# Down's first eight left factors in four rooms, and up's first two pairs in turn over T2 and T1

## The chip, the cores and the metric

The kernel runs on one core of one Trainium2 chip. The metric is device time of one execution in microseconds (us), from the first to the last instruction with what the runtime puts around it. Five engines work side by side, each through its own row of instructions in a fixed order: TensorE (PE in the profile; its weight loads are PEld), VectorE (DVE), ScalarE (ACT), GpSimd (POOL) and SyncE (SP, which only issues transfers here). They wait for each other by semaphores.

## What is computed

Two layers over 1024 positions of width 1024, all in float32. Each layer has a mixer (a recurrent one in layer 0, attention in layer 1) and then a feed-forward part with a causal convolution of three taps. The change touches only the second:

```python
def conv_ffn(x, w_up, conv_w, conv_b, w_down):
    hid = causal_dwconv(x @ w_up, conv_w, conv_b)      # 1024 -> 2 x 2816
    gate, val = jnp.split(hid, 2, axis=-1)
    return (jax.nn.gelu(gate) * val) @ w_down          # 2816 -> 1024
...
    x = x + rms_norm(mix, g[1])
    h = rms_norm(x, g[2])
    x = x + rms_norm(conv_ffn(h, ffn_w_up[l], ...), g[3])
```

## The kernel before

**A float32 product in three.** Each float32 number is split into a high part (a cast on ScalarE) and a low part (the number less the high part, on DVE or POOL). `mm3` then makes a product of three matmuls of 128x512: high by high (L187), high by the low part of the moving side (L188), low part of the weights by high (L189). So the high parts are wanted first, the low parts one and two matmuls later. The split stands at several lines: L395 and L396 in `combined` for factors of the weights of up, L436 and L437 in `split_k` for the operands T, L481 and L482 for the products made ahead, L183 and L184 in `split` for the factors of down.

**Seven products for eight.** Both matrix products of the feed-forward part are taken as 2 by 2 blocks with seven products in place of eight. The price is sums and differences of blocks: the operands T1 to T4 of the normalized input, the factors s1 = a21 + a22, s2 = s1 - a11, a11 - a21 and a12 - s2 of the weights (`mixed`, L401, s1 and a11 - a21 on POOL, the others on DVE), and in down differences of blocks of w_down (L659) and of the hidden part (L540 to L543 in `sums`).

**up** works through 22 blocks n of 128 gate or value channels, a gate and its value in turn. For the first six (`AHEAD`), two of the seven products need only the first half of the input. They are made ahead, while the norm of the second half is still under way ("the products made ahead", L476 to L496), for three pairs of blocks one after another: four weight tiles of a pair are cast on ScalarE, their low parts are made on DVE, and the results are parked in DRAM. After that a block n < 6 has five products: y by T2, a copy of y to u2 (ScalarE, L579), z by T1, a copy q, y by T3, `second()` (a sum of y and q on DVE, L568), z by b22, `third()` (L572), y by T4. Then follow the convolution (L461 on ScalarE, two taps on DVE at L463), gelu on ScalarE (L615), the product of gate and value (L621) and `sums`. T2 and T1 are made before the first block, T3, b22 and T4 from inside it (`rest`, L526). A block n from 6 on has seven products. Its factors are asked for one block ahead (`factors(n + 1)`, `ahead()`).

**down** is 6 x 11 and then some more steps of 12 matmuls. A step has a left factor, 128x512 of the hidden part, read back from DRAM (`fetch`, tiles ar) and split, and a right factor from w_down (tiles hl). `make` prepares steps in order, three ahead of the step that runs, and starts with the loads (SP), then the difference of w_down (L659), then the split of the left and of the right factor. The left factors of the first four steps have rooms of their own in a large tile called ring, from the pool of large tiles (four of them, `hpool`); it is taken before the last blocks of up. From step 4 on the left factor goes to one of four rooms called al, which are taken when down opens its rooms (`open_rows`), after the last sums of up.

Besides the loops, the tile scheduler fixes each engine's order when the program is built, so that an instruction of another line can come to stand ahead of or behind the one written first. What stands in the rows around the change is shown below.

Of the kernel before, what the change touches and what calls it, by code (L numbers as in the profile page):

```python
# [26 lines left out]
FT = DFF // P  # L27
# [13 lines left out]
def hybrid_kernel(  # L41
# [56 lines left out]
    def bank(name):  # L98
        return psp.tile([P, HT], F32, tag="b4", name=name, bufs=4)

    def pj():
        return psp.tile([P, HT], F32, tag="pj", name="pj")
# [285 lines left out]

    def combined(raws, begun):

# [12 lines left out]

        s1 = mixed(pool, a21, a22, ALU.add)
        if begun:
            s2 = mixed(dve, s1, a11, ALU.subtract)
            yield split_of(s2, dve)
            yield split_of(s1, dve)
            yield split_of(mixed(pool, a11, a21, ALU.subtract), dve)
            yield split_of(mixed(dve, a12, s2, ALU.subtract), dve)  # L410
            yield split_of(a22, dve)
            return
# [9 lines left out]
    def up(l, hb, load_first, begin_down):  # L422
# [15 lines left out]

        def raw(f, s, i):
            own = s == 0 and "uraw" in pools  # L440
            name = "uraw" if own else "raw"
            t = (pools["uraw"] if own else rawp).tile([P, 4, P], F32, tag=name, name=name)
            nc.sync.dma_start(out=t, in_=w_up[l, s * FT + f, i].rearrange("p (k c) -> p k c", k=4))
            return t
# [30 lines left out]
        for n in range(0, AHEAD, 2):  # L475
            ws = [[], []]  # L476
            for i in range(2):
                for e, f in enumerate(order[n : n + 2]):
                    a = raw(f, 0, i)
                    w = wp.tile([P, 2, 4, P], F32R, tag="hl", name="hl")  # L480
                    act.copy(w[:, 0], a)  # L481
                    dve.tensor_tensor(out=w[:, 1], in0=a, in1=w[:, 0].bitcast(F32), op=ALU.subtract)  # L482
                    ws[e].append(w)
# [16 lines left out]
        def factors(n):  # L500
            f = order[n]
            return combined([raw(f, s, i) for s in range(2) for i in range(2)], n < AHEAD)

        ws = factors(0)
        early = [next(ws) for _ in range(2)]
        t2, t1, b22 = (operand(True) for _ in range(3))
# [20 lines left out]
        others = rest()  # L527
        next(others)

# [16 lines left out]
        def begin(n):  # L546
# [4 lines left out]
            return p1, c1  # L551

        g0 = None
        for n, f in enumerate(order):
            if n == FT - 4:
                load_first()
            more = factors(n + 1) if n + 1 < FT else begin_down()
            take, nxt = iter(early), []

            def ahead():  # L560
                nxt.append(next(more))

            y, z = pj(), bank("z")
            u2, q, c2 = tap("u2"), tap("q"), room("c")

            def second():

                dve.tensor_tensor(out=c2[:, first[1]], in0=y, in1=q, op=ALU.add)  # L568

# [4 lines left out]
            if n < AHEAD:  # L574
                p1, c1 = begin(n)
                act.copy(y, p1)
                w = next(ws)
                product(y, next(take), t2, False)
                act.copy(u2, y)  # L579
                w2 = next(ws)  # L580
                product(z, next(take), t1, True)
                act.copy(q, z)
                w3 = next(ws)
                next(others, None)
                product(y, w, t3, False)
                second()
                ahead()
                next(others, None)
                product(z, w2, b22, False)
                third()  # L590
                ahead()
                next(others, None)
            else:
# [23 lines left out]
            act.copy(c2[:, first[0]], y)  # L617
            if n + 1 >= AHEAD:
                ahead()
# [6 lines left out]
    def down(l, xsrc, dst, tail, primed):  # L626
# [76 lines left out]
        def make():  # L703
# [19 lines left out]
            r = raws.pop(i)  # L723
            a = st["ring"][:, i] if i < 4 else st["al"][i % 4]
            w_ = r.shape[-1]
# [1006 lines left out]
```

## Time and profile before

| | |
|---|---|
| median of 3 runs | 2436.53 us (2436.25 to 2438.01) |
| the profiled execution | 2437.43 us |
| its span, first to last instruction | 2435.7 us (1.73 around it) |
| granted TensorE clock, mean | 0.986 |
| busy: PE, PEld | 2328.8 us (96%), 1905.0 us (78%) |
| busy: DVE, ACT, POOL | 1917.9 us (79%), 1320.2 us (54%), 390.3 us (16%) |
| instructions | 32154 |
| moved by DMA | 279.08 MB, mean 115 GB/s |

Some places on the profile's clock, counted from the span's start: in layer 0 the products made ahead begin at 439.6, T2's first difference on DVE at 470.4, down with its first matmuls before 899.3; in layer 1 the same are at 1759.3, 1786.0 and before 2214.3.

A row of a timeline has the start, the duration, engine, line and operation, then the tile written, the tiles read (buffer numbers left out), their shape, and the count of instructions that the row takes together. In square brackets stands the idle time before it and what ended it. The granted clock (PEclk) is 1.00 where TensorE ran at full pace. A matmul's duration is longer than its distance to the next one, since matmuls overlap in the pipeline.

### The profile page before, as it was taken

To read this page: it belongs to the slowest core of one execution; us is meant where nothing else is said; L and a number is where in the kernel's file an instruction comes from. 1 tells how busy PE (TensorE), PEld (TensorE's weight loads), DVE (VectorE), ACT (ScalarE), POOL (GpSimd) and SP (SyncE) were. 2 spreads that over 40 slices of the span, in tenths; PEclk is the share of its full clock that TensorE was granted. 3 is DMA by queue.
4 is the path that set the end of the run, shared out by engine and by line. 5 is a ranking of instruction groups with operands and counts; after the bars stand their busy time and mean duration, and the time that the engine had idled before them with its cause. 6 is when DMAs were issued, how large, how long until landed. Compare 5 with 4: busy or idle time off the path is not lost.

```text
span 2435.7 us, 32154 instructions
## 1 busy us (share of the span) xinstructions
PE 2328.8 (96%) x10998; PEld 1905.0 (78%) x10998; DVE 1917.9 (79%) x3376; ACT 1320.2 (54%) x2440; POOL 390.3 (16%) x275
## 2 busy tenths in 40 slices
PE   8999999989999999998989999989989999999997
PEld 6888777767888878887778888877767788887886
DVE  6576776898888889586788888886988888887776
ACT  5343674655555545564556565565665555554453
POOL 2000000122333310000111111132031333330000
PEclk9999999999999999999999999999999999999999
DMA  4111125753233265433221121134665232237342
GB/s 140 35 33 38 40 80 169 242 171 119 92 120 113 91 206 172 129 124 120 64 54 45 50 53 52 52 90 126 229 200 180 98 119 104 91 122 262 113 152 94
DMA packets 145220, 279.08 MB, mean 115 GB/s; under 512 B 17600, under 2 KB 30048, under 8 KB 145056
## 3 DMA queue, kind: packets, MB, share of 16 engines
q1 hardware_dynamic: 143472, 272.66, 34.9%
q0 software_dynamic: 1440, 4.38, 0.6%
q8 instruction: 86, 1.41, 0.3%
q14 instruction: 78, 0.64, 0.1%
q10 hardware_dynamic: 144, 0.00, 0.0%
HBM read 200.36 MB, written 68.22 MB: 110 GB/s over the span
## 4 chain that ended last, share of the span: by engine, by line
PE 51%; DVE 15%; ACT 4%; issue 4%; DMA 2%; POOL 1%; SPq 0%; ACTq 0%; DVEq 0%; POOLq 0%
PE pj L187 8%; PE pj L189 8%; PE pj L188 8%; PE z L187 4%; PE z L189 4%; PE z L188 4%; PE x L189 2%; PE x L187 2%; DVE nm L1443 2%; PE x L188 2%; ACT pl L1453 2%; DVE pt L184 2%; PE tr L189 1%; PE tr L187 1%; PE tr L188 1%
## 5 line engine op out<-in xcount | busy, mean ns | idle before, releaser
L187 PE MATMUL pj<-op,hl 128*128 128x512 f32 x704 | 280.0, 398 | 18.8 <-ACT u L579 9.9
L188 PE MATMUL pj<-op,hl 128*128 128x512 f32 x704 | 278.2, 395 | 6.6 <-DVE op L437 6.4
L189 PE MATMUL pj<-op,hl 128*128 128x512 f32 x704 | 277.2, 394 | 3.4 <-DVE hl L482 3.4
L463 DVE SCALAR_TENSOR_TENSOR y<-c,cw,y 128x1023 f32<-128x1023 f32 (+1 forms) x176 | 230.6, 1311 | 6.4 <-ACT y L461 4.8
L187 PE MATMUL pj<-hh,hl 128*128 128x512 f32 x544 | 228.4, 420 | 0.3 <-DVE offs L1290 0.3
L189 PE MATMUL pj<-hh,hl 128*128 128x512 f32 x544 | 213.7, 393 | 0.0
L188 PE MATMUL pj<-hl,hl 128*128 128x512 f32 x544 | 213.6, 393 | 0.0
L183 ACT CAST al<-ar 128x512 fp32r<-128x512 f32 (+2 forms) x179 | 95.9, 543 | 173.8 <-PE z L188 48.1
L396 DVE TENSOR_TENSOR hl<-ws,hl 128x512 fp32r<-128x512 f32 x176 | 128.3, 731 | 69.3 <-ACT hl L395 69.1
L187 PEld LDWEIGHTS pj<-op,hl 128*128 128x128 f32 x704 | 133.5, 190 | 54.5 <-ACT u L579 13.9
L178 ACT CAST hl<-raw 128x512 fp32r<-128x512 f32 x173 | 106.5, 621 | 123.9 <-PE dn L189 39.8
L184 DVE TENSOR_TENSOR al<-ar,al 128x512 fp32r<-128x512 f32 (+2 forms) x179 | 104.1, 588 | 79.7 <-ACT al L183 79.3
L188 PEld LDWEIGHTS pj<-op,hl 128*128 128x128 f32 x704 | 133.7, 190 | 37.6 <-DVE op L437 10.9
L189 PEld LDWEIGHTS pj<-op,hl 128*128 128x128 f32 x704 | 133.9, 190 | 32.7 <-DVE hl L482 4.6
L395 ACT CAST hl<-ws 128x512 fp32r<-128x512 f32 x176 | 108.7, 620 | 92.2 <-PE pj L189 78.0
L401 POOL TENSOR_TENSOR ws<-raw 128x512 f32<-128x512 f32 x44 | 76.3, 1734 | 444.6 <-DMA raw<-in_w_up_dram 384.5
L179 POOL TENSOR_TENSOR hl<-raw,hl 128x512 fp32r<-128x512 f32 x56 | 73.0, 1304 | 462.2 <-ACT hl L178 444.9
L401 POOL TENSOR_TENSOR ws<-uraw,raw 128x512 f32<-128x512 f32 x44 | 91.9, 2088 | 288.6 <-DVE hl L396 274.3
L187 PE MATMUL z<-op,hl 128*128 128x512 f32 x352 | 137.7, 391 | 0.0
L188 PE MATMUL z<-op,hl 128*128 128x512 f32 x352 | 137.5, 391 | 0.0
L189 PE MATMUL z<-op,hl 128*128 128x512 f32 x352 | 137.2, 390 | 0.0
L179 DVE TENSOR_TENSOR hl<-raw,hl 128x512 fp32r<-128x512 f32 x117 | 80.9, 700 | 63.6 <-ACT hl L178 63.3
(459 smaller groups left out, 6412.3 us busy)
## 6 DMA issues: line engine op xcount, KB each, us to landing
raw<-in_w_up_dram SPq DMA_DIRECT2D x112, 256.0 KB
uraw<-in_w_up_dram SPq DMA_DIRECT2D x88, 256.0 KB
ar<-s SPq DMA_DIRECT2D x88, 256.0 KB
raw<-in_w_out_dram SPq DMA_DIRECT2D x87, 256.0 KB
wd<-in_w_down_dram SPq DMA_DIRECT2D x64, 256.0 KB
mid<-y SPq DMA_DIRECT2D x24, 512.0 KB
xt<-mid SPq DMA_DIRECT2D x24, 512.0 KB
raw<-in_w_qkv_dram SPq DMA_DIRECT2D x48, 256.0 KB
```

The lines of the kernel that those rows point to most:

```text
L178: act.copy(hl[:, 0], raw)
L179: (pool if low[0] else dve).tensor_tensor(out=hl[:, 1], in0=raw, in1=hl[:, 0].bitcast(F32), op=ALU.subtract)
L183: act.copy(hi, src)
L184: dve.tensor_tensor(out=lo, in0=src, in1=hi.bitcast(F32), op=ALU.subtract)
L187: pe.matmul(o, wh, xh, start=start, stop=False, skip_group_check=taps)
L188: pe.matmul(o, wh, xl, start=False, stop=False, skip_group_check=taps)
L189: pe.matmul(o, wl, xh, start=False, stop=stop, skip_group_check=taps)
L395: act.copy(w[:, 0], src)
L396: eng.tensor_tensor(out=w[:, 1], in0=src, in1=w[:, 0].bitcast(F32), op=ALU.subtract)
L401: eng.tensor_tensor(out=t, in0=a, in1=b, op=op)
L463: dve.scalar_tensor_tensor(out=y[:, d:], in0=c[:, : T - d], scalar=cw[:, 2 - d, ch : ch + 1], in1=y[:, d:], op0=ALU.mult, op1=ALU.add,)
L1443: dve.tensor_reduce(out=nm[:, x0 : x0 + 1], in_=lg[:, :n], axis=AX.X, op=ALU.max, negate=True)
```

## The change

Five edits, all for both layers.

1. Of the products made ahead, the four low parts of the first pair (n == 0) are made on POOL and no longer on DVE.
2. The factors of the first two blocks are asked for together ahead of T2, and their sums s1 and a11 - a21 are made on DVE and no longer on POOL. The fourth raw tile of block 1 goes to the pool uraw.
3. Blocks 0 and 1 run in turn: y by T2 for both, then z by T1 for both, then the rest of block 0 and the rest of block 1. T1 is split after the two products by T2.
4. In block 1, `second()` has ScalarE copy y to c2, and DVE adds q to that copy. Before, DVE read y itself.
5. In down the left factors of steps 4 to 7 go into the ring's four rooms a second time, and al begins with step 8.

```diff
-    def combined(raws, begun):
+    def combined(raws, begun, busy=pool):
...
-        s1 = mixed(pool, a21, a22, ALU.add)
+        s1 = mixed(busy, a21, a22, ALU.add)
         if begun:
             s2 = mixed(dve, s1, a11, ALU.subtract)
             yield split_of(s2, dve)
             yield split_of(s1, dve)
-            yield split_of(mixed(pool, a11, a21, ALU.subtract), dve)
+            yield split_of(mixed(busy, a11, a21, ALU.subtract), dve)
...
-        def raw(f, s, i):
-            own = s == 0 and "uraw" in pools
+        def raw(f, s, i, own=None):
+            own = "uraw" in pools and (s == 0 or own)
...
-                    dve.tensor_tensor(out=w[:, 1], in0=a, in1=w[:, 0].bitcast(F32), op=ALU.subtract)
+                    (dve if n else pool).tensor_tensor(out=w[:, 1], in0=a, in1=w[:, 0].bitcast(F32), op=ALU.subtract)
...
-            return combined([raw(f, s, i) for s in range(2) for i in range(2)], n < AHEAD)
-
-        ws = factors(0)
-        early = [next(ws) for _ in range(2)]
+            raws = [raw(f, s, i, n == s == i == 1) for s in range(2) for i in range(2)]
+            return combined(raws, n < AHEAD, dve if n < 2 else pool)
+
+        made = [factors(n) for n in range(2)]
+        lead = [next(w) for w in made]
...
+        begun = []
+        for n in range(2):
+            p1, c1 = begin(n)
+            y = pj()
+            act.copy(y, p1)
+            begun.append([y, bank("z"), tap("u2"), tap("q"), c1])
+        for (y, _, u2, _, _), w in zip(begun, lead):
+            product(y, w, t2, False)
+            act.copy(u2, y)
+        next(others)
+        lead = [next(w) for w in made]
+        for n, (_, z, _, q, _) in enumerate(begun):
+            product(z, lead[n], t1, True)
+            act.copy(q, z)
+            lead[n] = next(made[0])
+            next(others)
...
             def second():
 
-                dve.tensor_tensor(out=c2[:, first[1]], in0=y, in1=q, op=ALU.add)
+                o = y
+                if n == 1:
+                    o = c2[:, first[1]]
+                    act.copy(o, y)
+                dve.tensor_tensor(out=c2[:, first[1]], in0=o, in1=q, op=ALU.add)
...
-            a = st["ring"][:, i] if i < 4 else st["al"][i % 4]
+            a = st["ring"][:, i % 4] if i < 8 else st["al"][i % 4]
```

Lines move with it: L659 of before is L693 after, L621 is L655, L579 is L614, L582 is L617, L615 is L649. A number behind a tile's name tells its buffers apart, and the same tile can have another number in the two programs.

DVE at the start of down in layer 0, before: the lows of the right factors (hl) and the last sums of the hidden part stand in turn, and the first low of al stands behind differences of w_down.

```order
L621 TENSOR_TENSOR y_7276<-y_7276,y_7299 128x1024
L184 TENSOR_TENSOR hl_7375<-wd_6685,hl_7375 128x512
L540 TENSOR_TENSOR y_7110<-y_7110,y_7276 128x512
L184 TENSOR_TENSOR hl_7397<-wd_6685,hl_7397 128x512
L541 TENSOR_TENSOR y_7110<-y_7110 128x512
L184 TENSOR_TENSOR hl_7418<-wd_6685,hl_7418 128x512
L543 TENSOR_TENSOR c_7146<-y_7276,y_7110 128x512
L659 TENSOR_TENSOR wd_6685<-wd_7433,wd_6685 128x512
L184 TENSOR_TENSOR hl_7440<-wd_6685,hl_7440 128x512
L659 TENSOR_TENSOR wd_6685<-wd_7433,wd_6685 128x512 x6
L184 TENSOR_TENSOR al_7334<-ar_7238,al_7334 128x512
```

The same place after:

```order
L655 TENSOR_TENSOR y_7277<-y_7277,y_7300 128x1024
L184 TENSOR_TENSOR ring_7230<-ar_7239,ring_7230 128x512
L540 TENSOR_TENSOR y_7111<-y_7111,y_7277 128x512
L184 TENSOR_TENSOR hl_7376<-wd_6686,hl_7376 128x512
L541 TENSOR_TENSOR y_7111<-y_7111 128x512
L184 TENSOR_TENSOR ring_7230<-ar_7241,ring_7230 128x512
L543 TENSOR_TENSOR c_7147<-y_7277,y_7111 128x512
L184 TENSOR_TENSOR hl_7398<-wd_6686,hl_7398 128x512
L184 TENSOR_TENSOR ring_7230<-ar_7243,ring_7230 128x512
L184 TENSOR_TENSOR hl_7419<-wd_6686,hl_7419 128x512
L184 TENSOR_TENSOR ring_7230<-ar_7368,ring_7230 128x512
L184 TENSOR_TENSOR hl_7441<-wd_6686,hl_7441 128x512
```

The lows of the left factors of steps 4 to 7 (ring) have moved in between the last sums and stand ahead of all seven differences of w_down, which follow as one run.

ScalarE in up, layer 0, from the convolution of block 1 to the copies of block 2, before (y is the convolution's tile, pj the accumulator y of a block, p1 the parked first product):

```order
L576 COPY pj_4414<-p1_4419 128x512
L395 CAST hl_4426<-ws_4424 128x512
L461 ACTIVATE y_4377<-c_4298,cw0_232 128x1024
L617 COPY c_4296<-pj_4292 128x512
L395 CAST hl_4444<-ws_4442 128x512
L461 ACTIVATE y_4395<-c_4296,cw0_232 128x1024
L615 ACTIVATE y_4377<-y_4377 128x1024
L579 COPY u2_4416<-pj_4414 128x512
```

And after:

```order
L611 COPY pj_4416<-p1_4420 128x512
L395 CAST hl_4427<-ws_4425 128x512
L599 COPY c_4340<-pj_4172 128x512
L461 ACTIVATE y_4378<-c_4169,cw0_232 128x1024
L651 COPY c_4340<-pj_4172 128x512
L461 ACTIVATE y_4396<-c_4340,cw0_232 128x1024
L614 COPY u2_4418<-pj_4416 128x512
L649 ACTIVATE y_4378<-y_4378 128x1024
```

The copy u2 of block 2 stood behind the gelu of block 1 and now stands ahead of it. L599 is the added copy of block 1.

ScalarE at the products made ahead in layer 1, before; L481 casts the weights (four of a pair), L259 squares the rows of the second half of the input for its norm:

```order
L481 CAST hl_16514<-raw_16512 128x512
L481 CAST hl_16585<-raw_16583 128x512
L495 COPY c1_16553<-x_16518 128x512
L481 CAST hl_16590<-raw_16588 128x512
L259 ACTIVATE ht_16465,ss_16464<-y1_16433 128x1024
L481 CAST hl_16595<-raw_16593 128x512
L259 ACTIVATE ht_16467,ss_16464<-y1_16435 128x1024
```

And after:

```order
L481 CAST hl_16515<-raw_16513 128x512
L259 ACTIVATE ht_16466,ss_16465<-y1_16434 128x1024
L495 COPY c1_16554<-x_16519 128x512
L259 ACTIVATE ht_16468,ss_16465<-y1_16436 128x1024
L481 CAST hl_16586<-raw_16584 128x512
L481 CAST hl_16591<-raw_16589 128x512
```

The casts of the second pair (hl_16586 and on), of which two stood ahead of the first square, now stand behind both squares.

More of the change, by code (lines that the diff above doesn't have):

```diff
@@ L527, in up @@
         others = rest()
-        next(others)
         def sums(n, g0, gt, c):
@@ L556, in up @@
                 load_first()
-            more = factors(n + 1) if n + 1 < FT else begin_down()
-            take, nxt = iter(early), []
+            if n == 0:
+                ws, more = made
+                w, w2 = lead
+            elif n == 1:
+                more = factors(2)
+            else:
+                more = factors(n + 1) if n + 1 < FT else begin_down()
+                take = iter(early)
+            nxt = []
             def ahead():
                 nxt.append(next(more))
-            y, z = pj(), bank("z")
-            u2, q, c2 = tap("u2"), tap("q"), room("c")
-            def second():
-                dve.tensor_tensor(out=c2[:, first[1]], in0=y, in1=q, op=ALU.add)
+            c2 = room("c")
+            if n < 2:
+                y, z, u2, q, c1 = begun[n]
+            else:
+                y, z, u2, q = pj(), bank("z"), tap("u2"), tap("q")
+            def second():
+                o = y
[3 more added lines that the diff above has]
+                dve.tensor_tensor(out=c2[:, first[1]], in0=o, in1=q, op=ALU.add)
             def third():
@@ L574, in up @@
             if n < AHEAD:
[L575 to L583, printed above, removed]
+                if n == 1:
+                    w, w2, w3 = early
+                elif n:
+                    p1, c1 = begin(n)
+                    act.copy(y, p1)
+                    w = next(ws)
+                    product(y, next(take), t2, False)
+                    act.copy(u2, y)
+                    w2 = next(ws)
+                    product(z, next(take), t1, True)
+                    act.copy(q, z)
+                if n != 1:
+                    w3 = next(ws)
                 next(others, None)
@@ L587, in up @@
                 ahead()
-                next(others, None)
                 product(z, w2, b22, False)
@@ L591, in up @@
                 ahead()
-                next(others, None)
             else:
@@ L617, in up @@
             act.copy(c2[:, first[0]], y)
-            if n + 1 >= AHEAD:
+            if n == 0 or n + 1 >= AHEAD:
                 ahead()
```

## The prediction

> **What bounds the kernel now.** I read the page's busy times first, then tables of windows by stage, then the timelines and waits of the three places that the change touches. The first line is the page's share of each engine; then five windows, with the columns us, busy (count) of PE, PEld, DVE, ACT and POOL, granted clock, DMA share, GB/s.
>
> ```profile
> PE 2328.8 (96%) x10998; PEld 1905.0 (78%) x10998; DVE 1917.9 (79%) x3376; ACT 1320.2 (54%) x2440; POOL 390.3 (16%) x275
> ```
>
> ```profile
> 930.00:950.00 20.00, 20.00 (x90) 16.57 (x89) 20.00 (x35) 8.87 (x16) 0.00 (x0) 1.00 0.45 138
> 899.32:911.37 12.05, 6.81 (x18) 4.77 (x16) 10.39 (x18) 3.31 (x7) 0.54 (x1) 0.72 0.93 312
> 2214.31:2225.50 11.19, 5.97 (x16) 4.12 (x15) 9.89 (x17) 2.48 (x5) 0.54 (x1) 0.69 0.95 319
> 470.44:579.23 108.79, 97.21 (x392) 75.28 (x391) 101.77 (x107) 61.96 (x89) 32.01 (x15) 0.94 0.50 168
> 1785.97:1894.60 108.63, 95.47 (x397) 73.87 (x395) 100.43 (x108) 62.27 (x90) 34.74 (x15) 0.97 0.52 168
> ```
>
> TensorE is the bound over the whole, so only a hole in its row can be won. Where nothing holds it, 90 matmuls fall into 20 us, two of them over an edge: 88 starts, one every 0.227 us; a step of down, or a product of up, of 12 matmuls takes 2.72 us. The change touches three places where this pace is missed, each in both layers: the start of down (899 and 2214), the first six blocks of up (470 to 579, 1786 to 1895; there DVE is busy 94% and 92%), and the first products of up, made ahead (440 and 1760 to 1770).
>
> **Start of down.** TensorE (PE), then what ran elsewhere meanwhile.
>
> ```profile
> 899.32 0.39 PE L189 MATMUL tr<-hl,ring 128*128 128x512 f32 x1
> ...
> 905.68 0.80 PE L189 MATMUL pj<-hl,al 128*128 128x512 f32 x1 [4.01 <-DVE al L184]
> 906.28 0.63 PE L187 MATMUL pj<-hl,al 128*128 128x512 f32 x1
> ...
> 2220.65 0.80 PE L189 MATMUL pj<-hl,al 128*128 128x512 f32 x1 [3.99 <-DVE al L184]
> ```
>
> ```profile
> 899.54 0.68 DVE L543 TENSOR_TENSOR c<-y 128x512 f32<-128x512 f32 x1
> 901.34 3.69 DVE L659 TENSOR_TENSOR wd<-wd 128x512 f32<-128x512 f32 x6
> 900.27 1.66 ACT L183 CAST al<-ar 128x512 fp32r<-128x512 f32 x3
> 910.25 1.14 ACT L183 CAST al<-ar 128x512 fp32r<-128x512 f32 x2 [8.31 <-DMA ar<-a]
> 903.10 2.88 SPq L693 DMA_DIRECT2D ar<-a  x2
> ```
>
> Step 3 ends at 899.32 with the fourth room of the ring. Step 4 takes its left factor from `al`, whose rooms come free only when the last sums of the hidden part are out (899.54); ScalarE casts at 900.27, and the low part stands on DVE behind six differences that end at 905.03. TensorE waits 4.01 us for it and then runs slowly, 0.63 a matmul against 0.39, with 0.72 as the stage's granted clock. From 899.32 to 911.37 sixteen starts follow, 16 x 0.227 = 3.6, so 12.05 - 3.6 = 8.4 us are lost; in layer 1 fourteen starts: 11.19 - 3.2 = 8.0.
>
> The edit lets steps 4 to 7 use the ring's four rooms again. Room i is free when step i has ended: steps of 2.72 us before 899.55 give rooms 0 to 3 at about 891.4, 894.1, 896.8 and 899.6. The casts and lows of steps 4 to 7 then stand on DVE among the last hidden sums. Spaced by 0.60 us (six differences in the 3.69 of 901.34) they are ready by my count at 897.2, 899.6, 901.4 and 902.7, and the right factors at 898.4, 900.8, 902.0 and 903.3; TensorE wants them at 899.6, 902.3, 905.0 and 907.7. So the whole 8.4 + 8.0 = 16.4 us goes, and with it the slow matmuls. What is late next is step 8, the first in `al`. Its load was issued as ar at 903.10 or after, in a stretch where the DMA engines are 93% busy; its low is due at 910.9 and DVE reaches it at about 910.0, by the same pitch, behind the differences moved down. That leaves 0.9 us. The four lows put ahead delay the last hidden sums by 1.2 us, which no one on TensorE waits for. I take off 0.4 for small waits: **16.0**, bounds 12 (step 8 late by 4.4 over both layers) and 16.4.
>
> **First six blocks of up.** Pitches of DVE, its rows beside GpSimd (POOL), the waits of this window in layer 0 (total, times, longest), and one late wait of TensorE.
>
> ```profile
> 516.55 1.27 DVE L396 TENSOR_TENSOR hl<-ws,hl 128x512 fp32r<-128x512 f32 x2
> 484.06 2.35 DVE L437 TENSOR_TENSOR op<-hb,op 128x1024 fp32r<-128x1024 f32 x2
> 527.42 1.28 DVE L463 SCALAR_TENSOR_TENSOR y<-c,cw,y 128x1022 f32<-128x1022 f32 x1
> 481.95 9.14 POOL L401 TENSOR_TENSOR ws<-raw 128x512 f32<-128x512 f32 x1 [6.37 <-DVE hl L396]
> 489.88 2.29 DVE L437 TENSOR_TENSOR op<-hb,op 128x1024 fp32r<-128x1024 f32 x1
> 501.36 1.29 POOL L401 TENSOR_TENSOR ws<-raw 128x512 f32<-128x512 f32 x1 [8.05 <-DVE hl L396]
> 501.53 2.19 DVE L437 TENSOR_TENSOR op<-hb,op 128x1024 fp32r<-128x1024 f32 x1 [0.26 <-ACT op L436]
> ```
>
> ```profile
> PE pj L187 <- ACT u L579: 5.2, 4, 2.1
> PE pj L188 <- DVE op L437: 2.8, 2, 1.8
> PE pj L187 <- ACT op L436: 2.3, 2, 1.5
> DVE ws L401 <- POOL ws L401: 2.4, 2, 1.2
> DVE c L568 <- PE pj L189: 0.9, 1, 0.9
> ```
>
> ```profile
> 573.37 0.80 PE L187 MATMUL pj<-op,hl 128*128 128x512 f32 x1 [2.08 <-ACT u L579]
> 576.09 0.63 PE L187 MATMUL pj<-op,hl 128*128 128x512 f32 x1
> ```
>
> In line, a DVE instruction of 128x512 takes 0.60 us, one of 128x1024 1.14, a conv tap 1.20. In the 107 of the first window stand 64, 23 and 20 of them: 38.4 + 26.2 + 24.0 = 88.6 us. Busy is 101.8, so 13.2 us went where DVE stood still beside POOL: an L437, 1.14 in line, took 2.19 while POOL's sum of 501.36 ran, another 2.29 at 489.88. Fifteen POOL instructions, 0.88 each; the remaining 108.8 - 101.8 = 7.0 are waits.
>
> The change takes four POOL sums per layer away and gives DVE four of 0.60. Of the first four POOL sums I find 1.1 us of lost DVE time each (the rows at 489.88 and 501.53 less 1.14), 4.3. The wait of 0.9 for TensorE at the first second() goes with the first pairs run in turn, whose order gives T2 and T1 four products in a row, and 0.3 for ScalarE. So DVE by itself gains 4.3 - 2.4 + 1.2 = 3.1. TensorE can gain more: from n=2 on, ScalarE now makes the copy u2 ahead of gelu, and gelu waits for DVE's conv. That releases TensorE's 5.2 us for u2, and the half pace from 573.37 to 576.09 (six starts later, 2.72 instead of 1.36), 6.6 in all, as far as DVE's splits let it run ahead, since it is 94% busy up to there. I take 5.0, between 3.1 and 6.6, since TensorE becomes the bound from the seventh block on: **10.0** for both layers. Bounds per layer: -2.4 (four more on DVE, no lock less), and 10.3, all three waits of TensorE above. The added ScalarE copy at n=1 (0.59) waits for y's third product; behind it stand the conv and the casts of n=2, and DVE's add waits for it. Bare it costs 0.59 + 0.60 once a layer; I take it as covered, since by then DVE has its queue of splits to work through. The loads of the first two pairs are issued earlier on SP; the DMA share of 0.50 covers them.
>
> **First products of up.** First TensorE, DVE and ScalarE in layer 0, then layer 1.
>
> ```profile
> 443.28 0.50 PE L189 MATMUL pj<-op,hl 128*128 128x512 f32 x1 [3.10 <-DVE hl L482]
> 446.96 0.46 PE L189 MATMUL pj<-op,hl 128*128 128x512 f32 x1
> 439.80 1.21 DVE L437 TENSOR_TENSOR op<-hb,op 128x1024 fp32r<-128x1024 f32 x1
> 438.54 0.61 ACT L481 CAST hl<-raw 128x512 fp32r<-128x512 f32 x1
> 1757.09 0.60 ACT L481 CAST hl<-raw 128x512 fp32r<-128x512 f32 x1
> 1768.08 0.39 PE L189 MATMUL x<-op,hl 128*128 128x512 f32 x1
> 1771.29 0.50 PE L189 MATMUL pj<-op,hl 128*128 128x512 f32 x1 [0.33 <-DVE hl L482]
> 1772.36 0.16 DVE L249 TENSOR_SCALAR ss<-ss 128x2 f32<-128x2 f32 x1
> ```
>
> The third matmul of the first product waits 3.10 us for a low part at the end of DVE's queue; up to 446.96 ten starts follow 439.80, so 7.16 - 2.3 = 4.9 us are lost. On POOL the low can start when ScalarE has the high part, 439.15, and takes 1.29 as POOL's sum of 501.36: ready at 440.4, or, if the L437 of 439.80 goes first, 441.0 + 1.3 = 442.3. The matmul is due at 440.0, so 0.4 to 2.3 us stay. Less a wait of up to 2 us for the next block's low, +2 (bounds -3.4, if that low takes the 9.14 us of POOL's sum at 481.95 and is ready at 448.3, and 4.5). In layer 1 there was hardly a wait (0.33); after, the high parts of n=2 stand behind two squares and its lows behind the L249 that waits for them (over at 1772.5 before), 1.5 us after the due time of 1771.0, less the 0.3 of now: -1.2 (bounds 0.3 and -7, a low of 9.14 from 1757.7 for a matmul due three products ahead of 1768.1). Together **+0.8**.
>
> After a wait of 2.08 us the matmuls from 573.37 ran at half pace for 2.7 us; in the 2.3 us case that costs another 1.4. [...]
>
> **The rivals.**
>
> *Step 8 takes over the wait (8%).* The 0.9 us margin is thin, loads run at 93% DMA share, and the cast at 910.25 had waited for DMA. Then 16.0 goes to 0: 2437.4 - 10.8 = 2426.6 on the profiled run, 2425.7 on the median.
>
> *TensorE runs free in up (12%).* If u2 and the T waits all go, 10 per layer: 10 x 2 + 16.8 = 36.8, 2437.4 - 36.8 = 2400.6. DVE at 94% speaks against it.
>
> *Up gives all back (10%).* DVE stays the pacer, and 2.4 us more work meets as many locks; 2437.4 - 16.8 = 2420.6.
>
> *Slower: POOL's four lows are starved (3%).* The sum at 481.95 took 9.14 us beside a DVE queue without a gap, until L437 at 489.88. If each of four lows took d, layer 0 would have them at 439.15 + 4d against a due time of 440.0 + 3 x 2.72 = 448.2, less the 4.9 lost now: 4d - 14; layer 1 at 1757.7 + 4d against 1768.1: 4d - 10.4. It eats the other 26 us when 8d - 24.4 = 26, d = 6.3. At 9.14 it costs 49: 2437.4 - 26 + 49 = 2460. Against it: DVE's queue in the pre-block has many 128x2 instructions with gaps. A milder form, half of it, gives 2436 (3%).
>
> [...]
>
> That the change doesn't do what it says has 2%: the order of the rows shows the ring's lows and the pairs in turn.
>
> **How the numbers follow.** 16.0 + 10.0 + 0.8 = 26.8. The profiled run took 2437.43, 0.9 above the median of 2436.53; 2437.43 - 26.8 - 0.9 = 2409.7, rounded 2410. My forecast has 62%. The range, on the median, 2398 to 2426: the low end is TensorE free in up and 2 us more at the first products, the high end the case of step 8. Below 2431.7 is faster by over 0.2% (4.9 us), about what a measurement here can tell: forecast, three faster rivals and half of the doing-nothing leave 0.93, same 0.04, slower 0.03.
>
> **What would show it.** In the profile after: in down no wait of 4 us for `al` at step 4, the granted clock there near 1, and the first `al` wait at step 8; in up POOL sums fewer by four before the third block, u2's wait for n=2 to 5 gone and second() of n=5 about 3 to 5 us earlier; L189 of the first product waiting 0.4 to 2.3 us for POOL. I am wrong if step 8 waits over 1 us for its low, if POOL's L482 takes over 3 us, or if TensorE still waits for u2.

## The result and the profile after

The median went from 2435.68 us (6 runs) to 2417.7 us (6 runs): the ratio is 0.9925, 95% interval 0.9913 to 0.9938, or 18.3 us less (15.1 to 21.2; the two medians differ by 18.0). The forecast was 26.8 us less. The profiled execution after is the shortest of its six: 2413.46 us, span 2411.7, where the other five lie between 2416.4 and 2419.6.

The page's first line for the kernel after has the busy times of before within 1 us for DVE and ScalarE; POOL is 7 us less busy, and TensorE 12 us, which goes with fewer slow matmuls (the granted clock is 0.993, 0.986 before):

```profile
PE 2316.6 (96%) x10998; PEld 1897.7 (79%) x10998; DVE 1918.4 (80%) x3376; ACT 1320.8 (55%) x2442; POOL 383.1 (16%) x275
```

To see where the time went I divided both traces at the same matmuls on TensorE. These are the dividing rows after: the first product made ahead, the first matmul behind the last turn of the normed rows (L279; taken as the start of up), the first step of down, a fixed place late in down, and the same in layer 1.

```profile
438.42 0.39 PE L187 MATMUL pj<-op,hl 128*128 128x512 f32 x1
467.34 0.48 PE L187 MATMUL pj<-op,hl 128*128 128x512 f32 x1
878.82 0.39 PE L187 MATMUL pj<-hl,ring 128*128 128x512 f32 x1
1055.73 0.47 PE L187 MATMUL pj<-hl,al 128*128 128x512 f32 x1
1742.98 0.40 PE L187 MATMUL pj<-op,hl 128*128 128x512 f32 x1
1773.85 0.48 PE L187 MATMUL pj<-op,hl 128*128 128x512 f32 x1
2185.62 0.39 PE L187 MATMUL pj<-hl,ring 128*128 128x512 f32 x1
```

The differences of neighbouring rows are the second column; the first is worked out in the same way from before's rows (439.57, 470.62, 887.91, 1071.55, 1759.27, 1786.15, 2202.87). The third is a further execution of the same changed kernel, "again" among the experiments.

| stretch, us | before | after | again | forecast of the change |
|---|---|---|---|---|
| products made ahead, layer 0 | 31.05 | 28.92 (-2.1) | 28.92 (-2.1) | -2 |
| up, layer 0 | 417.29 | 411.48 (-5.8) | 411.52 (-5.8) | -5 |
| down, layer 0, to the fixed place | 183.64 | 176.91 (-6.7) | 176.73 (-6.9) | -8 |
| products made ahead, layer 1 | 26.88 | 30.87 (+4.0) | 32.07 (+5.2) | +1.2 |
| up, layer 1 | 416.72 | 411.77 (-5.0) | 411.44 (-5.3) | -5 |
| down, layer 1, to the end | 232.83 | 226.08 (-6.8) | 229.19 (-3.6) | -8 |
| the six together | | -22.4 | -18.5 | -26.8 |

Outside of these stretches the span is 1.6 us shorter in the one trace and 1.1 us longer in the other; among the traces of this study (all but the one at a low clock, below) the time up to the first product made ahead differs by up to 2.8 us and the time from the fixed place in down to layer 1 by up to 6.6, with no change in either. So the two traces account for 18.5 to 22.4 us, which overlaps the interval of the medians.

**Down.** TensorE after, layer 0, at the first steps that use al, the only waits there:

```profile
901.99 0.50 PE L187 MATMUL pj<-hl,al 128*128 128x512 f32 x1 [0.51 <-ACT al L183]
902.33 0.40 PE L188 MATMUL pj<-hl,al 128*128 128x512 f32 x1
903.38 0.50 PE L189 MATMUL pj<-hl,al 128*128 128x512 f32 x1 [0.65 <-DVE al L184]
```

The wait of 4.01 us at step 4 is gone, with the slow matmuls. Step 8, the first in al, waits twice for about half a microsecond.

**Up.** The three largest waits of TensorE after, in the stretch from 468 to 575 of layer 0 (total, times, longest), then this stretch in both layers as windows with the columns of the prediction's:

```profile
PE pj L187 <- DVE c L600: 4.3, 3, 1.7
PE pj L187 <- ACT c L599: 2.9, 1, 2.9
PE pj L188 <- DVE op L437: 1.7, 2, 1.3
```

```profile
467.20:574.00 106.80, 96.71 (x409) 76.39 (x408) 104.15 (x116) 64.52 (x92) 24.10 (x12) 0.98 0.54 180
1773.00:1880.00 107.00, 96.48 (x408) 76.34 (x407) 103.55 (x115) 64.80 (x94) 24.31 (x12) 0.98 0.53 180
```

No wait for u2 is left. In its place TensorE waits for second() (L600) in blocks 3 to 5 and once for the new copy (L599). DVE is now busy 97%, and POOL 24 us in place of 32. All waits of TensorE in the stretch together went from 11.5 to 10.1 us in layer 0 and from 12.9 to 10.6 in layer 1. From about the 400th matmul of up on, both traces run alike, one matmul every 0.227 us.

**Products made ahead, layer 1.** TensorE, then ScalarE, then DVE and POOL after:

```profile
1744.01 0.49 PE L189 MATMUL pj<-op,hl 128*128 128x512 f32 x1 [0.40 <-POOL hl L482]
1758.07 0.50 PE L187 MATMUL pj<-op,hl 128*128 128x512 f32 x1 [2.71 <-ACT hl L481]
```

```profile
1754.84 1.06 ACT L259 ACTIVATE ht<-y 128x1024 f32<-128x1024 f32 x1 [3.91 <-DVE y L371]
1757.41 1.13 ACT L481 CAST hl<-raw 128x512 fp32r<-128x512 f32 x2
```

```profile
1742.72 1.26 DVE L249 TENSOR_SCALAR ss<-ss 128x2 f32<-128x2 f32 x1
1744.89 0.92 DVE L154 SCALAR_TENSOR_TENSOR rc_m<-rc_m,ss 128x2 f32<-128x2 f32 x1
1747.18 1.25 DVE L153 TENSOR_TENSOR rc_m<-ry_m 128x2 f32<-128x2 f32 x1
1751.51 1.27 DVE L155 SCALAR_TENSOR_TENSOR ry_m<-rc_m,ry_m 128x2 f32<-128x2 f32 x1
1753.39 2.74 DVE L371 SCALAR_TENSOR_TENSOR y<-y,ry_m,xt 128x512 f32<-128x512 f32 x4
```

```profile
1741.56 2.39 POOL L482 TENSOR_TENSOR hl<-raw,hl 128x512 fp32r<-128x512 f32 x1 [59.53 <-ACT hl L481]
1747.11 1.29 POOL L482 TENSOR_TENSOR hl<-raw,hl 128x512 fp32r<-128x512 f32 x1 [1.31 <-ACT hl L481]
1751.01 1.74 POOL L482 TENSOR_TENSOR hl<-raw,hl 128x512 fp32r<-128x512 f32 x1 [2.61 <-ACT hl L481]
```

Each of the four tiny DVE instructions (two columns only) takes 0.14 to 0.17 us elsewhere; overlapping a POOL low (that beside 1744.89 runs from 1744.50 to 1745.80) it takes 0.92 to 1.27, 4.1 us more in all. They belong to the norm's work and stand in DVE's row ahead of L371; the squares (L259) wait for L371, and the casts of the second pair (1757.41) now stand behind both squares. TensorE waits 2.71 us for them. DVE is also spared four lows of 0.60, so by this sum it should be 1.7 us late. The second square starts 13.4 us after the first product (1756.36), 1.5 us later than before (11.9, 1771.13).

### The profile page after: what moved, and what is told of

It reads as the page before. It is cut to its first block, busy times and chain, and to the rows that moved or that the text cites. A ratio compares the mean times of both kernels' runs of the same rounds, so it can differ in the third digit from the quotient of the medians.

```text
span 2411.7 us, 32179 instructions
## 1 busy us (share of the span) xinstructions
PE 2316.6 (96%) x10998; PEld 1897.7 (79%) x10998; DVE 1918.4 (80%) x3376; ACT 1320.8 (55%) x2442; POOL 383.1 (16%) x275
## 4 chain that ended last, share of the span: by engine, by line
PE 68%; DVE 19%; issue 4%; ACT 4%; DMA 3%; SPq 1%; POOL 0%; DVEq 0%; ACTq 0%; POOLq 0%
PE pj L187 10%; PE pj L189 10%; PE pj L188 10%; PE z L189 4%; PE z L187 4%; PE z L188 4%; DVE y L463 2%; DVE nm L1477 2%; PE x L189 2%; PE x L187 2%; PE x L188 2%; ACT pl L1487 2%; DVE pt L184 2%; PE py L187 2%; PE py L189 2%
## 5 line engine op out<-in xcount | busy, mean ns | idle before, releaser
L463 DVE SCALAR_TENSOR_TENSOR y<-c,cw,y 128x1023 f32<-128x1023 f32 (+1 forms) x176 | 236.8, 1349 | 3.0 <-ACT y L461 1.8
L187 PEld LDWEIGHTS pj<-op,hl 128*128 128x128 f32 x704 | 132.9, 189 | 49.9 <-DVE c L600 11.1
L184 DVE TENSOR_TENSOR al<-ar,al 128x512 fp32r<-128x512 f32 (+2 forms) x171 | 98.6, 583 | 64.8 <-ACT al L183 63.7
L401 POOL TENSOR_TENSOR ws<-uraw,raw 128x512 f32<-128x512 f32 x40 | 85.8, 2145 | 266.8 <-DVE hl L396 259.6
L189 PEld LDWEIGHTS pj<-hh,hl 128*128 128x128 f32 x544 | 102.4, 188 | 23.2
```

Source lines behind the costliest of these rows:

```text
L184: dve.tensor_tensor(out=lo, in0=src, in1=hi.bitcast(F32), op=ALU.subtract)
L187: pe.matmul(o, wh, xh, start=start, stop=False, skip_group_check=taps)
L189: pe.matmul(o, wl, xh, start=False, stop=stop, skip_group_check=taps)
L401: eng.tensor_tensor(out=t, in0=a, in1=b, op=op)
L463: dve.scalar_tensor_tensor(out=y[:, d:], in0=c[:, : T - d], scalar=cw[:, 2 - d, ch : ch + 1], in1=y[:, d:], op0=ALU.mult, op1=ALU.add,)
```

## The experiments

My theory after this reading: POOL's lows pay in layer 0 and cost 4 to 5 us in layer 1; in up DVE paces, so that moving waits of TensorE about brings nothing; the ring's worth is cut by step 8. The rivals are in the expectations. A lock, in the expectations and in the prediction, is DVE's longer time beside POOL (in before an L437 of 1.14 us took 2.19 and 2.29; after, an instruction of the norm of 0.16 took 1.25); the traces show the longer times, and no run shows what holds DVE. Stretches are named as in the table.

**low_dve: all lows on DVE again.**

```diff
-                    (dve if n else pool).tensor_tensor(out=w[:, 1], ...)
+                    dve.tensor_tensor(out=w[:, 1], ...)
```

> The changed kernel with edit 1 undone in both layers: the four low parts of the first pair made ahead are on DVE again. Theory: in layer 0 the wait of the first product comes back (the changed kernel is 2.1 us shorter there than before); in layer 1 the four low parts on POOL cost 4.0 us from the first product made ahead to the start of T2, so without them that stretch is 26.9 us again and not 30.9. Together about 1.9 us faster than the changed kernel. Rival: the 4.0 us of layer 1 come from the pairs run in turn or from the earlier loads of their factors (edits 2 and 3), not from POOL; then the stretch of layer 1 stays at 30.9 us and the kernel is about 2 us slower than the changed one.

Measured: products made ahead 31.05 us in layer 0 and 28.25 in layer 1 (30.87 and 32.07 with the lows on POOL), up 410.99 and 411.60. Median 2415.98 us, ratio to before 0.992 (0.990 to 0.994). So layer 0's 2.1 us are edit 1's, and most of layer 1's loss too. In layer 1, 1.4 us over before's 26.88 stay in this run; the next one has the same order there and does not show them. In this run a cast of the first pair waits 2.8 us for its load, and the second square starts 13.4 us after the first product, as late as in the changed kernel; yet the second pair starts after 12.35 us, where it is 15.1 in the changed kernel and 11.1 before, since two of its casts stand ahead of the squares.

**low_l0: lows on POOL in layer 0 alone.**

```diff
-                    (dve if n else pool).tensor_tensor(out=w[:, 1], ...)
+                    (dve if n or l else pool).tensor_tensor(out=w[:, 1], ...)
```

> The changed kernel with the four low parts on POOL in layer 0 alone and on DVE in layer 1. Theory: layer 0 keeps its 2.1 us, layer 1 gets back its 4.0 us (stretch from the first product made ahead to T2 26.9 us); the span 4 us shorter than that of the changed kernel. Rival (edits 2 and 3 cause the 4.0 us): no change against the changed kernel, the stretch stays at 30.9 us.

Measured: 28.89 us in layer 0 and 26.90 in layer 1, as the theory has it; span 2404.3. Median 2413.29 us, ratio 0.9903 (0.9881 to 0.9924). This is the lowest median of the kernels that compute both layers in full. Its interval overlaps that of the changed kernel, so the 4 to 5 us are shown by the stretch, not by the medians. The other traces agree: the stretch takes 30.8 to 33.3 us in the seven traces with lows on POOL in layer 1, and 26.6 to 28.3 in the five without any work on POOL there.

**idle_pool_l1 and idle_pool_again: POOL busy, the lows not on it.** Added in layer 1, first pair, to low_l0:

```diff
+                    if l and not n:
+                        pool.tensor_tensor(out=half_slot("junk"), in0=a.rearrange("p k c -> p (k c)"), in1=a.rearrange("p k c -> p (k c)"), op=ALU.subtract)
```

> The kernel with low parts on POOL in layer 0 alone, and in layer 1 four extra POOL differences of the same shape beside the first pair, whose results nobody reads; the lows themselves stay on DVE, and the order of the casts on ScalarE stays the one with two casts of the second pair ahead of the squares. It tells two parts of the theory apart. If the locks count (DVE's 128x2 instructions of the norm took 1.25 us in place of 0.16 four times beside POOL's lows), the norm's chain in layer 1 is 3 to 4 us later, and the stretch from the first product made ahead to T2 takes 29 to 31 us. If only the order of the casts counts (casts of the second pair behind the two squares), the stretch stays within 1 us of 26.9.

> The kernel of idle_pool_l1 a second time, since all stages of its first run were longer, those without any change too. Expected as before: if POOL's locks on DVE's norm instructions count, the stretch from the first product made ahead to T2 in layer 1 takes 29 to 31 us; if only the order of the casts counts, it stays within 1 us of 26.9.

The first run had a granted clock of 0.848 over the whole kernel and took 2583.56 us; nothing is read from it. In the second the stretch in layer 1 took 29.86 us, 3.0 more than low_l0, with two casts of the second pair ahead of the first square, as before (the third, which stood between the squares, stands behind both). The time was 2420.86 us, one run. DVE and POOL:

```profile
1747.65 1.02 DVE L249 TENSOR_SCALAR ss<-ss 128x2 f32<-128x2 f32 x1
1749.18 1.01 DVE L148 TENSOR_SCALAR ry_m<-ss 128x2 int32<-128x2 int32 x1
1751.45 1.00 DVE L154 SCALAR_TENSOR_TENSOR rc_m<-rc_m,ss 128x2 f32<-128x2 f32 x1
```

```profile
1745.41 4.76 POOL L484 TENSOR_TENSOR junk<-raw 128x512 f32<-128x512 f32 x2 [59.18 <-DMA raw<-in_w_up_dram]
1751.38 1.05 POOL L484 TENSOR_TENSOR junk<-raw 128x512 f32<-128x512 f32 x1 [1.22 <-DMA raw<-in_w_up_dram]
```

Tiny DVE instructions of the norm again take 1.0 us where they overlap POOL, though nothing waits for POOL's results. So with POOL busy, and nothing else of edit 1, the stretch took 3.0 us more, in one trace. But TensorE loses them at other places than in the changed kernel: it waits 0.4 to 0.9 us at four products for lows that stand late in DVE's row, and for no cast. By this run the delay on DVE would have most of the 4.0 us and the order of the casts the rest; by low_dve, where squares as late cost 1.4 us in the old order, it is the other way round. Both follow from edit 1; how the 4.0 us divide between them stays open.

**no_ring and ring_alone: edit 5 taken out, and edit 5 alone.** The line of edit 5 as before in the one; that line alone added to the kernel before in the other.

> The changed kernel with edit 5 undone: al begins with step 4 again. Theory: the ring is worth 6.7 us per layer, so the waits of about 4 us and the slow matmuls come back, 13.5 us slower than the changed kernel. Rival: part of the 13.5 us came from edits 2 to 4, which end up earlier and so let the loads of down start earlier; then the loss here is under 10 us.

> The kernel before with edit 5 alone: ring for the first eight steps of down, nothing else. Theory: 6.7 us per layer, 13.5 us faster than before, with step 8 waiting about 1 to 1.6 us for the load of its right factor (we). Rival: 16.0 us as the prediction had it, step 8 without a wait.

Measured: without the ring down takes 183.88 and 232.45 us, as before within 0.4, and the median is 2426.81 us, ratio 0.9971 (0.9959 to 0.9983). With the ring alone down takes 177.13 and 226.24, and the median is 2423.42 us, ratio 0.9959 (0.9945 to 0.9972), 10 us less than before (7 to 13). In the traces the ring is worth 6.4 to 7.0 us per layer, whether or not the other edits are there (3.3 in layer 1 against "again"), and in the medians about 10 where 13.5 was expected. The rival of no_ring, a loss under 10 us because the other edits have a part in it, does not show in the traces; the medians do not rule it out (2426.81 against 2418.38 for "again", on the same chip).

What takes the rest is step 8. ScalarE after at that step, layer 0, then TensorE and ScalarE in "again", layer 1:

```profile
900.18 1.20 ACT L183 CAST hl<-we 128x512 fp32r<-128x512 f32 x2 [8.21 <-DMA we<-in_w_down_dram]
901.32 1.14 ACT L183 CAST al<-ar 128x512 fp32r<-128x512 f32 x2
```

```profile
2213.76 0.50 PE L187 MATMUL pj<-hl,al 128*128 128x512 f32 x1 [1.94 <-ACT al L183]
2215.69 0.63 PE L187 MATMUL pj<-hl,al 128*128 128x512 f32 x1
```

```profile
2211.83 1.28 ACT L183 CAST hl<-we 128x512 fp32r<-128x512 f32 x2 [9.07 <-PE tr L189]
2213.09 1.14 ACT L183 CAST al<-ar 128x512 fp32r<-128x512 f32 x2
```

In ScalarE's row the casts of the right factors of steps 8 and 9 (we) come first; the cast of step 8's left factor (al) stands behind them. What it waits for is its own load. SyncE issues that load behind the two of we, and by the trace's record of landings it is complete at 901.30 in layer 0, 0.02 us before the cast at 901.32; in layer 1 of "again" it is complete at 2213.07, before the cast at 2213.09. Eleven traces have the ring for eight or twelve steps; in 20 of their 22 layers the cast starts within 0.03 us of the landing of its load. The issue of the load in layer 0 (SPq):

```profile
894.94 0.37 SPq L727 DMA_DIRECT2D ar<-a  x1
```

The load takes 6.4 us with the DMA engines busy 91% from 894.94 to 901.30, and 7.4 us in layer 1 of "again" (issued at 2205.68). The first wait of TensorE at step 8 in layer 1 is 0.35 us in one execution of the changed kernel and 1.94 in another, and after the 1.94 the matmuls take 0.63 us each for a while (2215.69). With the half pace that is the 3.1 us by which down of layer 1 differs between the two (226.08 and 229.19).

**ring_12: the ring for twelve steps**, on top of low_l0.

```diff
-            a = st["ring"][:, i % 4] if i < 8 else st["al"][i % 4]
+            a = st["ring"][:, i % 4] if i < 12 else st["al"][i % 4]
```

> The kernel with low parts on POOL in layer 0 alone, and with the ring used for the first twelve steps of down and not eight; al begins with step 12. Theory: the 1.2 to 1.6 us that TensorE still waits at step 8 come from the casts of the left factor standing behind those of the right factor, whose load (we) lands at 900.2; with the left factor's cast and low ahead of it, at most 0.5 us stay, and the stretch from the first step of down on is about 1 us shorter per layer (176.9 and 226.1 in the changed kernel). Rival: the load of the right factor alone sets the wait; no change.

Measured: the edit did not bring about the order that the expectation speaks of. In both layers, by the rooms in the program as built, the cast that moved ahead of those of we is that of step 9; step 8's stays behind them. ScalarE in layer 0, then in layer 1:

```profile
900.78 0.62 ACT L183 CAST hl<-we 128x512 fp32r<-128x512 f32 x1 [2.81 <-DMA we<-in_w_down_dram]
901.70 0.62 ACT L183 CAST hl<-we 128x512 fp32r<-128x512 f32 x1 [0.29 <-DMA we<-in_w_down_dram]
902.53 0.62 ACT L183 CAST ring<-ar 128x512 fp32r<-128x512 f32 x1 [0.22 <-DMA ar<-a]
```

```profile
2201.27 1.36 ACT L183 CAST hl<-we 128x512 fp32r<-128x512 f32 x2 [4.66 <-DMA we<-in_w_down_dram]
2202.62 0.62 ACT L183 CAST ring<-ar 128x512 fp32r<-128x512 f32 x1
```

Step 8 waits 0.23 + 0.36 us in layer 0, and 1.68 + 0.59 in layer 1. Down takes 176.38 us in layer 0, 0.5 less than in the changed kernel, but 227.45 in layer 1, 1.4 more, so the microsecond per layer did not come. Median 2413.43 us, ratio 0.9917 (0.9898 to 0.9936), beside 0.9903 for low_l0, on which it builds: no gain. The rooms called al are thus not what is late at step 8. In layer 0 the cast visibly waits for its load (ar), after the casts of we were done; in layer 1 the load is complete at 2202.60, and the cast follows at 2202.62. So neither the theory nor the rival held: it is the load of the left factor itself. Issuing it ahead of the loads of we was not tried.

**copy_all and no_copy: who paces up.** Edit 4 in blocks 1 to 5, and in none.

```diff
-                if n == 1:
+                if 1 <= n < AHEAD:      # copy_all
+                if n < 0:               # no_copy
```

> The changed kernel with the ScalarE copy of edit 4 in blocks 1 to 5 and not in block 1 alone. In the changed kernel TensorE waits 1.2, 1.4 and 1.7 us per layer for second() on DVE in blocks 3 to 5 (and for u2 no more). Theory: DVE is the late engine there and a copy on ScalarE frees y sooner, so these 4.3 us per layer go, up to 8 us faster in all. Rival: DVE paces the stage, so TensorE's wait only moves to the splits or to T operands; within 2 us of the changed kernel. Second rival: the copy stands behind gelu again, as in block 1, and each costs about what that one costs: 2 to 4 us slower per block.

> The changed kernel with edit 4 undone: in block 1 DVE reads y itself in second(), and ScalarE makes no copy. In the changed kernel TensorE waits 2.9 us for that copy, which stands behind gelu of block 0, and runs at half pace for 4 us after (4.6 us lost per layer together). Theory: DVE's add stands one instruction of 1.21 us and itself behind third(), so y comes free at 511.5 and not at 509.9; the wait grows to about 4.5 us and the kernel is 1 to 4 us slower per layer. Rival: the copy is what makes the wait, since ScalarE is the late engine; without it the wait shrinks under 2.9 us and the kernel is up to 4 us faster per layer.

Measured: with the copy everywhere up takes 411.59 and 411.48 us, against 411.48 and 411.77. TensorE in copy_all, layer 0:

```profile
550.44 0.50 PE L187 MATMUL pj<-op,hl 128*128 128x512 f32 x1 [3.15 <-ACT u L614]
551.76 0.63 PE L188 MATMUL pj<-op,hl 128*128 128x512 f32 x1
```

All three waits for second() are gone, and one wait of 3.15 us for u2, in layer 0 with slow matmuls after it, has come in their place: the first rival. Median 2415.61 us, ratio 0.9929 (0.9913 to 0.9946). Without any copy the wait in block 1 is 4.61 us for DVE instead of 2.90 for ScalarE, and up takes 412.98 and 413.07, 1.3 to 1.5 us longer per layer, as the theory said, though in layer 1 another trace with the copy has 412.86. The whole took 2417.3 us, one run, no longer than the changed kernel.

**one_tap: 14.4 us less of DVE per layer**, one tap of the convolution left out in the first six blocks.

```diff
-            for d in (1, 2):
+            for d in (1,) if f in order[:AHEAD] else (1, 2):
```

> The changed kernel with one of the two taps of the convolution on DVE left out in the first six blocks of up (12 instructions of 1.2 us per layer, 14.4 us of DVE; the output is no longer the reference's). Theory: DVE paces this stage, and TensorE's waits there (14.5 us lost per layer) are all DVE's lateness; the stretch from T2 to down is 6 to 12 us shorter per layer than in the changed kernel (411.5 and 411.8). Rival: the waits of TensorE belong to the order on ScalarE (the copy behind gelu, u2), and DVE's time is cover; then the stretch is less than 2 us shorter.

Measured: up 404.33 and 403.80 us, 7.2 and 8.0 less, about half of the DVE time taken out; 2405.37 us, one run. Some of the waits that are left in layer 0, and the window:

```profile
PE pj L188 <- DVE op L437: 1.6, 2, 1.3
PE pj L187 <- DVE c L600: 1.0, 2, 0.8
PE pj L187 <- ACT u L614: 0.6, 1, 0.6
```

```profile
468.00:566.00 98.00, 93.25 (x399) 73.93 (x398) 91.17 (x105) 63.44 (x90) 17.23 (x12) 1.00 0.58 192
```

With DVE at 93% the wait for the copy of block 1 (L599) is gone as well, though nothing on ScalarE was changed. In the changed kernel ScalarE itself waits to make it, and not for gelu, which was over at 506.7. ScalarE, then DVE, after:

```profile
505.63 1.06 ACT L649 ACTIVATE y<-y 128x1024 f32<-128x1024 f32 x1
...
509.28 0.58 ACT L599 COPY c<-pj 128x512 f32<-128x512 f32 x1 [1.55 <-DVE y L463]
```

```profile
507.92 1.27 DVE L463 SCALAR_TENSOR_TENSOR y<-c,cw,y 128x1022 f32<-128x1022 f32 x1
```

What it waits for is the end of block 0's second tap. That tap reads a c of block 0, and the copy writes a c of block 1. The pool has three rooms for c, and in the program as built these two have the same room and the copy is made to wait for this tap. What a fourth room would be worth was not tried. So the expectations of no_copy and copy_all, which put the copy's wait down to gelu, had the place wrong. DVE paces this stage: taking time off DVE shortens it, moving TensorE's waits does not.

**sums_pool: the sums of the first two blocks on POOL again.**

```diff
-            return combined(raws, n < AHEAD, dve if n < 2 else pool)
+            return combined(raws, n < AHEAD, pool)
```

> The changed kernel with the sums s1 and a11 - a21 of blocks 0 and 1 on POOL again (the second half of edit 2 undone); all else as in the changed kernel. Theory: those four POOL sums cost DVE 1.1 us each in locks and save it 0.6 each, so the stretch from T2's first matmuls to the seventh block is about 2 us longer per layer than in the changed kernel. Rival: the sum on POOL is starved for 8 to 9 us behind DVE's queue, as it was before, and the product by T1 of block 1 has to wait for its factor: 5 us or more longer per layer.

Measured: up takes 416.14 and 413.16 us, 4.7 and 1.4 longer, and the whole 2426.42 us, one run. None of the four sums took longer than 2.81 us on POOL, so the rival's starving did not happen; layer 1 is near the theory's 2 us. The layers differ by 3.3 us. In both DVE waits 1.2 us for POOL's sum and 1.8 for a cast; TensorE waits 6.2 us for second() in layer 0 and 3.8 in layer 1. Why stays open.

**again: the changed kernel once more.**

> The changed kernel once more, unchanged, as the measure beside the other three on one chip. Theory: the same stages within 1 us (first products of layer 1 at 30.9 us where before has 26.9), between 15 and 21 us faster than before.

Measured: the third column of the table. Median 2418.38 us, ratio 0.993 (0.9915 to 0.9946). The products made ahead in layer 1 differ from the first trace by 1.2 us and down of layer 1 by 3.1, more than expected. The 1.2 us are matmuls at half pace: in both traces TensorE waits 2.7 us for the same cast, but only in this one eight starts after it are slow.

## Why the prediction was right or wrong

**Down, 16.0 forecast, 13.5 and 10.5 in the two traces.** The mechanism was right: the room for al was the wait, and with the ring steps 4 to 7 run through. The term was mis-sized at step 8. The prediction named the operand, step 8's left factor, and saw that its load runs in a stretch with busy DMA engines, but its margin of 0.9 us counted the low on DVE alone, and no time for the load. The load took 6.4 us and was complete at 901.30, when TensorE was about to run dry (it stood idle from 901.48). The rival "step 8 takes over the wait" happened in part, 2.5 us in one trace and 5.5 in the other, by the load and not by the low; the size changes from run to run. The prediction's sign of being wrong, over 1 us for the low, did not come (0.6 us); the longer wait was for the cast before it.

**Up, 10.0 forecast, 10.8 and 11.1 measured.** That DVE paces the stage was shown by one_tap and copy_all. That the size came out right is luck, since several terms were wrong and nearly cancelled. The added copy was "taken as covered"; TensorE waits 2.9 us for it, because the copy in turn waits for a tap on DVE. Taking it out is no better (no_copy), so what is late is DVE and not the copy. And u2's 5.2 us did not just go: 4.3 us of waits for second() came in their place. DVE's own sum was off too. It gave 4.3 us back for DVE's longer times beside POOL. The operands' instructions did lose less (L437 takes 1.22 us on average in place of 1.47), but the taps of the convolution lose 3.3 us more (1.53 in place of 1.40), so over all its instructions in the first six blocks the net is about 2 us in layer 0 and 1 in layer 1. What DVE gained instead were its own waits, which the prediction put at 1.2 us: they fell from 9.9 to 5.3 us in layer 0 and from 10.9 to 5.5 in layer 1; those for ScalarE's casts, its convolution and TensorE are gone, and those for POOL's sums are 1.2 us in place of 2.4 and 5.0. On TensorE's side the waits for T fell (1.7 us for DVE's lows in place of 2.8 in layer 0, none of the 2.3 for ScalarE's casts), and the granted clock over the stage was 0.98 in place of 0.94 and 0.97; waits alone are 1.4 and 2.3 of the 5.8 and 5.0 us. Edit 3, the blocks in turn, was never tried by itself, so its share in up stays open.

**Products made ahead, layer 0, +2 forecast, 2.1 gained.** The first low was 0.83 us late (0.4 to 2.3 forecast) and the next pair's 1.45 (up to 2). POOL was not starved: its four lows, from 438.09 on, took 6.54 us together.

**Products made ahead, layer 1, 1.2 lost by the forecast, 4.0 and 5.2 measured.** This step failed, at two places. It saw that the casts of the second pair would stand behind both squares, but priced the low part, due at 1771.0. TensorE wants the high part first, two matmuls earlier:

```profile
1770.34 0.39 PE L187 MATMUL pj<-op,hl 128*128 128x512 f32 x1
```

That is 11.1 us after the first product; in the changed kernel the same matmul starts after 15.1, with the wait of 2.71 us for the cast. And the time of the squares and of L249 (1772.5) was taken from before's trace, though POOL's lows themselves make them 1.5 us later, through four tiny DVE instructions, each 0.8 to 1.1 us longer beside a POOL low. The prediction had priced DVE's longer times beside POOL in up (1.1 us for each of the first four sums) and forgot them here: at 1747.18 an instruction of 0.16 us took 1.25, beside a POOL instruction of 1.29 that began 0.07 us earlier. The direction of the rival "starved" was wrong: it was DVE that was held up, not POOL.

The sum is 22.4 or 18.5 us in the traces where 26.8 was forecast; the measured time lies inside the range, and the missing 4 to 8 us are 2.8 to 4 in layer 1's products and 2.5 to 5.5 at step 8, less about 1 more than forecast in up.

## What to carry to other kernels

When an instruction moves to GpSimd, look at what VectorE runs at that moment: in layer 1 here four tiny instructions beside POOL's lows took 0.8 to 1.1 us longer each, about as much as an L437 of 1024 columns beside a POOL sum (1.05 and 1.15 us longer, before). Look also at which instructions change their place on other engines by it: here the casts fell behind two squares. When a wait for a room is removed, price the next load as well: when it is issued, how long it takes while the transfer engines are busy (6.4 us here, at 91%), and when the step wants it. And in a stage that one engine paces, as DVE here at 97%, moving the waits of the others brought nothing (up took 411.59 and 411.48 us in copy_all, 411.48 and 411.77 in the changed kernel); what shortened it was less work on DVE (404.33 and 403.80 in one_tap) and fewer waits of DVE itself (9.9 us before, 5.3 after, in layer 0).

## What was not expected of the hardware

The same short wait of TensorE cost nothing more in one trace and was followed by a stretch at half pace in another. At step 8 of layer 1, sums_pool first, then low_dve (in both a second wait of 0.59 us follows two matmuls later):

```profile
2219.99 0.50 PE L187 MATMUL pj<-hl,al 128*128 128x512 f32 x1 [1.83 <-ACT al L183]
2222.33 0.63 PE L188 MATMUL pj<-hl,al 128*128 128x512 f32 x1
```

```profile
2210.49 0.50 PE L187 MATMUL pj<-hl,al 128*128 128x512 f32 x1 [1.84 <-ACT al L183]
2212.38 0.40 PE L188 MATMUL pj<-hl,al 128*128 128x512 f32 x1
```

After 1.83 us and the second wait the matmuls took 0.63 us each for about 2.5 us, one start every 0.43 us from 2221.91 to 2224.04; after 1.84 us and the second wait they took 0.40 at once, one start every 0.23 us. Nor did length tell the cases apart: after the 2.71 us of the products made ahead (the row at 1758.07) the next matmul took 0.40 us (1758.41), and after 2.70 us for the same cast in "again" (1760.72) they took 0.63. After the 2.90 us for the copy in up eight starts were 0.2 us late each in layer 0 of the changed kernel, and none in layer 1 of "again" (1820.20). In these traces half pace followed a wait of 2.08 us (573.37, before) and did not follow one of 3.12 us (1856.60, layer 1 of copy_all); it followed those of 3.15 us (550.44, copy_all), 3.99 and 4.01 us (before), and 4.03 and 4.04 us (no_ring). No run shows what decides it.
